# Seven half-size products in place of eight in a feed-forward up projection

## The chip, the cores and the metric

The kernel runs on one core of one Trainium2 chip. The metric is the device time of one launch in microseconds (us), the median of several runs. Lower is better.

## The reference, cut to what matters

The program is two transformer blocks on 512 tokens with 1024 features, in float32. The second block has two layers, and each layer ends with a feed-forward part:

```python
h = x + mixed @ w_out
f = jnp.square(jax.nn.relu(rmsnorm(h, norm2_g) @ w_up)) @ w_down
return h + f
```

`w_up` is 1024 by 4096 and `w_down` 4096 by 1024. The up projection thus has 32 output chunks of 128 features, each a contraction over eight chunks of 128, for 512 tokens.

## The kernel before, in words

Activations lie with features on partitions, so a tensor of 1024 features is eight tiles of 128 x 512. Each float32 operand is split into two float32r parts, H (a rounded copy, made by ScalarE, L140) and L (the rest, made by VectorE, L141). A product of two operands takes three matmuls: H by H, H by L, L by H (`mm3`, L162 to L164).

A weight chunk is loaded by one DMA of 512 KB from SyncE's queue (L150) into one of three `wr` buffers, split into one of two `w` buffers, and multiplied (`gemm`): eight contraction chunks, 24 matmuls of 512 columns. In the feed-forward part (`ffn`), the residual times the norm's gain is split once (`gain_split`, L229 and L230) into eight `x` buffer pairs. The norm's factor `rs` comes from `rstd_tile`: squares on ScalarE (L195), their sums on VectorE (L196), a few small matmuls, and twelve small VectorE operations (L123 to L134). Four groups follow. A group has eight up outputs and then eight down outputs, which take the group's eight up outputs as their contraction. An up output is read from PSUM by VectorE with max and times `rs` (L1910), squared by ScalarE (L1911) and split into a `y` buffer pair. A down output is added to the residual by VectorE (L1917).

Before the feed-forward part stands an output projection (L1895) whose eight results are added to `h` one by one (L1896). Its operand `mixed` lies in the same eight `x` buffer pairs, so these come free chunk by chunk while the last of its eight outputs is multiplied.

Buffers of a name (`w2` has eight, `wr` three, `w` two, `x` and `y` eight pairs, `wg` six) are handed out in program order. A planner (the Tile layer) then orders each engine's instructions: among those that are ready in its own model of time, the one that stands first in the program goes first. On the chip each engine runs its list in that order and waits on semaphores.

Of the kernel before, what the change touches and what calls it, by code (L numbers as in the profile page):

```python
# [49 lines left out]
class Builder:  # L50
    """Pools, constants and the operations that the stages share.

    Activations lie with features on partitions: a tensor of 1024 features is
    eight tiles of [128, 512 tokens]."""

    def __init__(self, tc, d, ctx):
# [3 lines left out]
        # whether the split of weights goes before all other work  # L60
# [31 lines left out]
    def psg(self):  # L92
        """In turn one of three banks; of two where attention takes the third."""
# [9 lines left out]
    def consts(self):  # L103
# [8 lines left out]
        # tri[s, l] = 1 where s <= l  # L112
# [6 lines left out]
    def rsqrt(self, out, x, scale, eps):  # L119
        """out = (scale * x + eps) ** -0.5 by Newton's steps, for small tiles."""  # L120
# [35 lines left out]
    def mm3(self, ps, wH, wL, xs, start=True, stop=True):  # L156
        """ps (+)= w.T @ x over the chunks, each operand in two parts."""
        nc = self.nc
        n = len(xs)
        for k, (xH, xL) in enumerate(xs):  # L160
            s, e = start and k == 0, stop and k == n - 1
            nc.tensor.matmul(ps, wH[:, k], xH, start=s, stop=False)  # L162
            nc.tensor.matmul(ps, wH[:, k], xL, start=False, stop=False)  # L163
            nc.tensor.matmul(ps, wL[:, k], xH, start=False, stop=e)  # L164
# [9 lines left out]
    def colsum(self, ps, acc, n=T):  # L174
        """ps[:, tb] = the sum over partitions of acc, tokens on partitions."""
# [4 lines left out]
    def rowbc(self, ps, col, n=T):  # L180
        """ps[p, t] = col[t % 128, t // 128] on every partition."""
# [17 lines left out]
    def rstd_rows(self, srcs, width, eps=EPS, n=T, w2=None, pss=None):  # L199
        """A PSUM tile with the tokens' reciprocal root mean squares on every partition."""  # L200
# [10 lines left out]
    def rstd_tile(self, srcs, width, eps=EPS, out=None):  # L211
        """The same on chip, until the next norm or in out."""
# [33 lines left out]
    def transpose4(self, ps, src, n=T):  # L246
        """ps[:, tb*128:...] = the transposes of src's blocks of 128 columns."""
# [5 lines left out]
    def causal_probs(self, score, mask, scale, pT):  # L253
        """The softmax of scale * (score + mask), keys on partitions: pT[k] holds for block k of
        keys the queries from that block on. score(ps, i) computes block i of queries against the
        keys up to it; mask[:, T - n:] is what is added to the last n keys up to a block's own."""
# [3 lines left out]
        def blocks(tile):  # L260
            # a block's columns in three tiles: the last, the first and third, the second
# [35 lines left out]
def fm(w):  # L297
    """[K, N] -> [N/128, 128, K/128, 128]: chunks of columns, contraction on partitions."""
# [8 lines left out]
def layout(x):  # L307
    """The program's arrays: the inputs, only laid out anew."""
# [12 lines left out]
    # S5: [(group parity, state), group pair, ...]  # L321
# [11 lines left out]
    # memory attention  # L333
# [3 lines left out]
    # PEER  # L337
# [4 lines left out]
    # second block  # L342
# [19 lines left out]
    # [layer, group of 8 chunks, out chunk, 128, 8, 128]  # L362
# [18 lines left out]
# columns of vec1  # L381
# [3 lines left out]
def exp_precise(B, out, x):  # L385
    """exp to float32's accuracy, for small tiles: 2**n times a polynomial."""
# [25 lines left out]
def pieces(x, bits, n):  # L412
    """x as a sum of float constants of few bits each, so that a product with a count is exact."""
# [13 lines left out]
def reduce_angle(B, x, tmp):  # L427
    """x - 2 pi round(x / 2 pi), within [-pi, pi]."""
# [31 lines left out]
def cmul(B, or_, oi, ar, ai, br, bi, t, neg_i=False):  # L460
    """(or_, oi) = (ar + i ai)(br + i bi); with neg_i the imaginary part is negated."""
# [14 lines left out]
class S5:  # L476
    """The state-space mixer: 8 steps of 64 chunks; (step, channel) on partitions for a
    group's input and output, (group parity, state) for the states. The groups go in
    quarters of 8, one tile of features each."""

    def __init__(self, B, pool):
# [15 lines left out]
        # powers 0..8  # L497
# [9 lines left out]
        # decay of eight steps; rotations of 8, 16, .. 256 steps  # L507
# [11 lines left out]
        # the factor of the input matrices, (A - 1) / lambda  # L519
# [14 lines left out]
    def matrices(self, q):  # L534
        """What a quarter's groups need of the parameters."""
# [25 lines left out]
        # output matrices C A^k, k = 0..8, the imaginary part negated  # L561
# [6 lines left out]
        # chunk inputs: A^(7-s) B, transposed to (step, channel) on partitions  # L568
# [13 lines left out]
        # kernels within a chunk: K_k[c', c] = Re(C A^k B), then laid out as a Toeplitz matrix  # L582
# [5 lines left out]
        # the two halves of the rows go to banks of their own  # L588
# [18 lines left out]
    def run(self, u, mats, outer):  # L607
        """u: a tile [(group, channel), (step, chunk)] -> gelu(y), laid out alike."""
# [17 lines left out]
        # rotate back, scan with real decays, rotate forth  # L626
# [35 lines left out]
def glu(B, yt, xs, vec):  # L662
    """Twice y * sigmoid(y @ w + b), in place."""
# [10 lines left out]
def glu_norm(B, yt, vec):  # L674
    """What glu gave, normalised; tokens back in their order; split."""
# [14 lines left out]
def attention_head(B, qT, kT, vt, h, out, pool):  # L690
    """A head of chunk-causal attention with a relative bias; out: the PSUM tile of its pair."""
# [3 lines left out]
    # the first chunk of a block doesn't see the second  # L695
# [13 lines left out]
def mixers(B, vec, memory, new_h):  # L709
    """The residual after the first block's mixers; memory() is a generator to run meanwhile."""  # L710
    nc, tc = B.nc, B.tc
    w = B.d["w_in"]
    with tc.tile_pool(name="mixers", bufs=1) as pool:
# [4 lines left out]
        # sel[k, n, p] = 1 where row k is the head of partition p in chunk n  # L718
# [12 lines left out]
        def ssm(p5):  # L731
# [42 lines left out]
        def pair(j):  # L774
            """The queries and keys of two heads, normalised."""
# [39 lines left out]
        def memories():  # L815
            # two steps a turn
# [22 lines left out]
        # the attention's part of the first products, meanwhile  # L839
# [22 lines left out]
def head_norms(B, raw, gains, per, width, n=T, w2=None, pss=None):  # L862
    """Scales each head's chunks (per of them) by its reciprocal root mean square and gains."""
# [17 lines left out]
def head_norm(B, raw, gains, width):  # L881
    """The same for one head; a generator."""
# [112 lines left out]
# products with experts' keys done while the gates are worked out  # L995
# [975 lines left out]
```

## Time and profile before

| what | value |
|---|---|
| median of 3 runs | 4764.99 us (4758.9 to 4768.86) |
| span of the profiled execution | 4766.1 us |
| TensorE busy | 4705.0 us (99%) |
| VectorE busy | 2838.4 us (60%) |
| ScalarE busy | 1907.6 us (40%) |

The span is what the chain of instructions takes in the one profiled execution; it lies 1.1 us above the median of the runs. [...]

### The profile page before, as it was taken

Reading aid. Unit: us, or ns where it says so; the run is one execution under the profiler, and the core shown is the slowest. Engines: PE = TensorE matmul, PEld = TensorE weight load, DVE = VectorE, ACT = ScalarE, POOL = GpSimd, SP = SyncE. Lnnn points to the kernel's source line nnn. Section 1 sums busy time; section 2 is a strip of 40 time slices with the busy share of each in tenths; the row PEclk is TensorE's granted clock in tenths of the full one; section 3 lists DMA queues with packets and bytes.
Section 4 is the critical chain, followed back from the end, with each engine's and each line's share of the span. In section 5 each row is a group of like instructions: output and inputs, shape, how many; then the busy total and the mean of one; then the engine's idle time right before and its main releaser. Section 6 shows DMA issues by size and latency. Waiting matters only on the chain.

```text
span 4766.1 us, 59356 instructions
## 1 busy us (share of the span) xinstructions
PE 4705.0 (99%) x22296; PEld 3754.0 (79%) x22296; DVE 2838.4 (60%) x5744; ACT 1907.6 (40%) x3653; POOL 29.1 (1%) x59
## 2 busy tenths in 40 slices
PE   8999999999999999999999999999999999999998
PEld 6777788888888888887787678888877876888887
DVE  8655799665545555557776545544477764555434
ACT  3343348863222222323553433333345534333322
POOL 0000000000000000000000000000000000000000
PEclk9789999999999999999999999999999999999999
DMA  4222235564434443442254145423323531554332
GB/s 131 66 84 83 80 118 186 190 210 150 138 119 139 143 129 126 145 138 74 85 178 137 45 154 175 146 93 96 104 81 127 174 103 52 176 167 133 93 95 82
DMA packets 306048, 589.28 MB, mean 124 GB/s; under 512 B 60192, under 2 KB 147552, under 8 KB 303584
## 3 DMA queue, kind: packets, MB, share of 16 engines
q1 hardware_dynamic: 304480, 582.88, 37.7%
q0 software_dynamic: 1280, 2.59, 0.3%
q8 instruction: 176, 2.88, 0.2%
q14 instruction: 112, 0.92, 0.1%
HBM read 480.29 MB, written 105.09 MB: 123 GB/s over the span
## 4 chain that ended last, share of the span: by engine, by line
PE 91%; DVE 6%; DMA 1%; issue 1%; ACT 0%; SPq 0%; DVEq 0%; ACTq 0%
PE g L162 14%; PE g L163 14%; PE g L164 14%; PE o L163 6%; PE o L164 6%; PE o L162 6%; PE s L1170 5%; PE s L1171 5%; PE s L1169 5%; PE s L1116 3%; PE s L249 1%; DVE wL L141 1%; PE s L1575 1%; PE s L1574 1%; PE s L183 1%
## 5 line engine op out<-in xcount | busy, mean ns | idle before, releaser
L140 ACT ACTIVATE wH<-wr 128x1024 fp32r<-128x1024 f32 (+2 forms) x599 | 603.3, 1007 | 1305.3 <-PE g L163 794.9
L141 DVE TENSOR_TENSOR wL<-wr,wH 128x1024 fp32r<-128x1024 f32 (+2 forms) x599 | 692.2, 1156 | 444.4 <-ACT wH L140 428.6
L162 PE MATMUL g<-xH,wH 128*128 128x512 f32 (+1 forms) x2328 | 923.4, 397 | 16.7 <-ACT wH L140 13.7
L164 PE MATMUL g<-xH,wL 128*128 128x512 f32 (+1 forms) x2328 | 919.9, 395 | 6.6 <-DVE wL L141 6.5
L163 PE MATMUL g<-xL,wH 128*128 128x512 f32 (+1 forms) x2328 | 922.2, 396 | 0.0
L162 PEld LDWEIGHTS g<-xH,wH 128*128 128x128 f32 x2328 | 444.7, 191 | 118.9 <-ACT wH L140 14.0
L164 PEld LDWEIGHTS g<-xH,wL 128*128 128x128 f32 x2328 | 444.4, 191 | 106.8 <-DVE wL L141 10.9
L163 PEld LDWEIGHTS g<-xL,wH 128*128 128x128 f32 x2328 | 444.7, 191 | 95.3 <-issue 3.7
L164 PE MATMUL o<-xH,wL 128*128 128x512 f32 x1032 | 411.2, 398 | 1.5 <-DVE wL L141 1.5
L163 PE MATMUL o<-xL,wH 128*128 128x512 f32 x1032 | 412.4, 400 | 0.0
L162 PE MATMUL o<-xH,wH 128*128 128x512 f32 x1032 | 411.2, 398 | 0.0
L1170 PE MATMUL s<-WL,VH 128*128 128x512 f32 x1024 | 399.7, 391 | 1.3 <-DVE WL L141 1.3
L1169 PE MATMUL s<-WH,VH 128*128 128x512 f32 x1024 | 398.2, 391 | 0.0
L1171 PE MATMUL s<-WH,VL 128*128 128x512 f32 x1024 | 397.7, 390 | 0.0
L140 ACT ACTIVATE VH<-vr 128x1024 fp32r<-128x1024 f32 x128 | 132.3, 1056 | 542.9 <-PE s L1170 391.4
L1172 DVE TENSOR_TENSOR h<-h,s 128x512 f32<-128x512 f32 x256 | 174.1, 685 | 271.6 <-PE s L1171 271.5
L164 PE MATMUL g<-yH,wL 128*128 128x512 f32 x632 | 251.0, 397 | 2.3 <-DVE wL L141 2.3
L163 PE MATMUL g<-yL,wH 128*128 128x512 f32 x632 | 251.1, 397 | 0.7 <-DVE yL L230 0.7
L162 PE MATMUL g<-yH,wH 128*128 128x512 f32 x632 | 250.5, 397 | 0.0
L141 DVE TENSOR_TENSOR VL<-vr,VH 128x1024 fp32r<-128x1024 f32 x128 | 154.1, 1224 | 141.4 <-ACT VH L140 141.3
L164 PEld LDWEIGHTS o<-xH,wL 128*128 128x128 f32 x1032 | 194.6, 189 | 45.2 <-DVE wL L141 2.4
L162 PEld LDWEIGHTS o<-xH,wH 128*128 128x128 f32 x1032 | 194.5, 188 | 44.5 <-issue 2.2
(629 smaller groups left out, 7243.3 us busy)
## 6 DMA issues: line engine op xcount, KB each, us to landing
wr<-in_w_in SPq DMA_DIRECT2D x166, 512.0 KB, 3.6
wr<-in_pu SPq DMA_DIRECT2D x128, 512.0 KB, 4.2
vr<-in_pv SPq DMA_DIRECT2D x128, 512.0 KB, 3.7
gd<-G SPq DMA_DIRECT2D x16, 2048.0 KB, 6.5
gt<-gd SPq DMA_DIRECT2D x64, 512.0 KB, 5.3
wr<-in_w_o SPq DMA_DIRECT2D x64, 512.0 KB, 3.6
wr<-in_w_up SPq DMA_DIRECT2D x64, 512.0 KB, 3.5
wr<-in_w_dn SPq DMA_DIRECT2D x64, 512.0 KB, 3.5
```

The source lines that it names most:

```text
L140: nc.scalar.activation(H, src, AF.Copy)
L141: nc.vector.tensor_tensor(L, src, f32(H), op=OP.subtract)
L162: nc.tensor.matmul(ps, wH[:, k], xH, start=s, stop=False)
L163: nc.tensor.matmul(ps, wH[:, k], xL, start=False, stop=False)
L164: nc.tensor.matmul(ps, wL[:, k], xH, start=False, stop=e)
L183: self.nc.tensor.matmul(ps[:, tb * P:(tb + 1) * P], col[:, tb:tb + 1].to_broadcast([P, P]), self.ident, start=True, stop=True)
L249: self.nc.tensor.transpose(ps[:, tb * P:(tb + 1) * P], src[:, tb * P:(tb + 1) * P], self.ident)
L1116: nc.tensor.matmul(ps[:, j * P:(j + 1) * P], o2[:, k], og[:, j], start=True, stop=True)
L1169: nc.tensor.matmul(ps, VH[:, n], WH, start=k == 0, stop=False)
L1170: nc.tensor.matmul(ps, VH[:, n], WL, start=False, stop=False)
L1171: nc.tensor.matmul(ps, VL[:, n], WH, start=False, stop=k == 3)
L1172: nc.vector.tensor_tensor(h[n], h[n], ps, op=OP.add)
```

## The change

The up projection goes two output chunks at a time (a pair). Seen as a 2 x 2 matrix of halves (outputs, contraction, tokens), a pair is eight products of half size. The change forms sums and differences of the quarters of the weights and of the operand and takes seven products (the Winograd form of Strassen's algorithm), whose sums give the four quarters of the result. `fast_moving` builds the operand's seven forms once for a layer. `fast_weights` builds the weights' four sums for each pair and splits seven half tiles. `fast_gemm` runs the seven products, each four contraction chunks of three matmuls of 256 columns: products 1, 3, 5 and 7 accumulate in PSUM bank x, 2 and 6 in bank y, 4 in bank z. Bank x is copied to SBUF by ScalarE after products 1, 3 and 5 (u0, u1, u2), and VectorE adds these copies to what lies in y and z. The down projection is as before. The rest of the textual change removes comments, so that line numbers shift.

```diff
+    def fast_moving(self, raws, main, extra):
...
+        for k in range(4):
+            r1, r2 = next(raws), next(raws)
+            t = self.w2(), self.w2()
+            t1, t2, t3, t4 = t[0][:, :n], t[0][:, n:], t[1][:, :n], t[1][:, n:]
+            v.tensor_tensor(t1, r1[:, n:], r1[:, :n], op=OP.subtract)
+            v.tensor_tensor(t3, r2[:, n:], r1[:, n:], op=OP.subtract)
+            v.tensor_tensor(t2, r2[:, n:], t1, op=OP.subtract)
+            v.tensor_tensor(t4, r2[:, :n], t2, op=OP.subtract)
+            A, Bt, E = main(), main(), extra()
+            for src, (H, L) in ((r1[:, :n], [x[:, :n] for x in A]), (t1, [x[:, n:] for x in A]),
+                                (r2, Bt), (t2, [x[:, :n] for x in E]), (t[1], [x[:, n:] for x in E])):
+                self.split(src, H, L)
...
+    def fast_weights(self, ap1, ap2, pool):
...
+            r.append(self.t([P, 8, P], F32, "wr", 3))
+            nc.sync.dma_start(r[-1], ap)
+        a11, a12, a21, a22 = r[0][:, :4], r[0][:, 4:], r[1][:, :4], r[1][:, 4:]
+        s = [self.w2().rearrange("p (k m) -> p k m", k=4) for _ in range(4)]
...
+            tag, home = (("w", None), ("v", pool))[i % 2]
+            H, L = (self.t([P, 8, P], F32R, tag + k, 2, home) for k in "HL")
...
+        v.tensor_tensor(s1, a21, a22, op=OP.add)
+        yield parts(0, a11, s1)
+        v.tensor_tensor(s2, s1, a11, op=OP.subtract)
+        yield parts(1, s2, a12)
+        v.tensor_tensor(s3, a11, a21, op=OP.subtract)
+        v.tensor_tensor(s4, a12, s2, op=OP.subtract)
+        yield parts(2, s3, s4)
+        yield parts(3, a22)
+
+    def fast_gemm(self, ap1, ap2, forms, part, tile, pool):
...
+        x, y, z = self.pss()[:, :n], self.pss()[:, :n], self.psg()[:, :n]
...
+        product(x, a, forms[0], True)
+        nc.scalar.copy(u[0], x)
+        product(y, b, forms[4], True)
+        a, b = next(w)
+        product(x, a, forms[5], False)
+        nc.scalar.copy(u[1], x)
+        product(z, b, forms[1], True)
+        v.tensor_tensor(c1[:, :n], z, u[0], op=OP.add)
+        a, b = next(w)
+        product(x, a, forms[6], False)
+        nc.scalar.copy(u[2], x)
+        v.tensor_tensor(c2[:, n:], y, u[2], op=OP.add)
+        (c,) = next(w)
+        product(y, b, forms[2], False)
+        v.tensor_tensor(c1[:, n:], y, u[1], op=OP.add)
+        product(x, c, forms[3], False)
+        return c1, (x, c2)
...
     def ffn(self, h):
...
-        xs = B.gain_split(h, vcol(self.vec, N2, 8), lambda: B.hl("x"))
+        with B.tc.tile_pool(name=f"ffn{self.l}", bufs=1) as pool:
+            self.ffn_in(h, pool)
...
+        def raws():
+            for k in (0, 4, 1, 5, 2, 6, 3, 7):
+                r = B.w2()
+                nc.scalar.activation(r, h[k], AF.Copy, scale=g8[k])
+                yield r
+        forms = B.fast_moving(raws(), lambda: B.hl("x"),
+                              lambda: [B.t([P, 3 * half], F32R, "xt" + k, 4, pool) for k in "HL"])
         rs = B.rstd_tile(h, 1024)
         for g in range(4):
             fs = []
-            for c in range(8):
-                ps = B.gemm(B.d["w_up2"][self.l, 8 * g + c], xs)
-                r, f = B.wg(), B.wg()
-                nc.vector.scalar_tensor_tensor(r, ps, 0.0, rs, op0=OP.max, op1=OP.mult)
-                nc.scalar.activation(f, r, AF.Square)
-                H, L = B.hl("y")
-                B.split(f, H, L)
-                fs.append((H, L))
+            for c in range(0, 8, 2):
+                w = [B.d["w_up2"][self.l, 8 * g + c + i] for i in range(2)]
+                c1, (x, c2) = B.fast_gemm(*w, forms, lambda: B.t([P, half], F32, "fu", 3, pool),
+                                           B.wg, pool)
+                for out, ps, sl in ((c1, c1, slice(0, T)), (c2, x, slice(0, half)),
+                                    (c2, c2[:, half:], slice(half, T))):
+                    nc.vector.scalar_tensor_tensor(out[:, sl], ps, 0.0, rs[:, sl], op0=OP.max, op1=OP.mult)
+                for r in (c1, c2):
+                    f = B.wg()
+                    nc.scalar.activation(f, r, AF.Square)
+                    H, L = B.hl("y")
+                    B.split(f, H, L)
+                    fs.append((H, L))
```

## Rows read from the trace of the kernel before

**Rows 1.** The page, part 1 (busy time by engine) and part 4 (chain by engine).
```profile
PE 4705.0 (99%) x22296; PEld 3754.0 (79%) x22296; DVE 2838.4 (60%) x5744; ACT 1907.6 (40%) x3653; POOL 29.1 (1%) x59
...
PE 91%; DVE 6%; DMA 1%; issue 1%; ACT 0%; SPq 0%; DVEq 0%; ACTq 0%
```

**Rows 2.** Windows: length, busy time of the engines, granted clock, DMA share, GB/s.
```profile
315.00:319.00 4.00, 4.00 (x19) 3.92 (x19) 0.00 (x0) 0.38 (x1) 0.00 (x0) 0.50 0.31 45
595.00:640.00 45.00, 44.70 (x218) 36.14 (x217) 44.59 (x251) 14.24 (x20) 0.00 (x0) 1.00 0.27 82
3120.00:3164.50 44.50, 44.50 (x196) 36.03 (x195) 20.67 (x27) 17.65 (x25) 0.00 (x0) 1.00 0.31 96
3164.50:3209.00 44.50, 44.50 (x193) 36.06 (x193) 15.31 (x16) 8.37 (x9) 0.00 (x0) 1.00 0.31 95
```

**Rows 3.** Timeline of PE: two matmuls of 512 columns, 24 matmuls apart.
```profile
3164.32 0.40 PE L162 MATMUL g<-yH,wH 128*128 128x512 f32 x1
...
3169.91 0.39 PE L162 MATMUL g<-yH,wH 128*128 128x512 f32 x1
```

**Rows 4.** Timeline of PE: matmuls of 256 columns, 15 matmuls apart.
```profile
302.42 0.28 PE L163 MATMUL g<-xL,wH 128*128 128x256 f32 x1
...
304.20 0.28 PE L163 MATMUL g<-xL,wH 128*128 128x256 f32 x1
```

**Rows 5.** Timeline of the weight loads of those matmuls, 15 loads apart.
```profile
302.42 0.19 PEld L164 LDWEIGHTS g<-xH,wL 128*128 128x128 f32 x1
...
304.20 0.19 PEld L164 LDWEIGHTS g<-xH,wL 128*128 128x128 f32 x1
```

**Rows 6.** Timeline of PE at a lower granted clock: 15 matmuls apart.
```profile
315.46 0.41 PE L163 MATMUL g<-xL,wH 128*128 128x256 f32 x1
...
318.66 0.41 PE L163 MATMUL g<-xL,wH 128*128 128x256 f32 x1
```

**Rows 7.** Timeline of DVE: three instructions that wait for nothing, 512 and 1024 columns.
```profile
3125.37 0.69 DVE L141 TENSOR_TENSOR yL<-wg,yH 128x512 fp32r<-128x512 f32 x1 [1.36 <-ACT yH L140]
3125.98 0.68 DVE L1910 SCALAR_TENSOR_TENSOR wg<-g,acc 128x512 f32<-128x512 f32 x1
3126.58 1.21 DVE L141 TENSOR_TENSOR wL<-wr,wH 128x1024 fp32r<-128x1024 f32 x1
```

**Rows 8.** Timeline of DVE: 256 columns, the first two reading PSUM.
```profile
171.52 0.41 DVE L633 TENSOR_TENSOR s5t<-s,roti 128x256 f32<-128x256 f32 x1
171.85 0.41 DVE L632 TENSOR_TENSOR s5t<-s,rotr 128x256 f32<-128x256 f32 x1
172.19 0.41 DVE L634 TENSOR_TENSOR s5t<-s5t,s5t 128x256 f32<-128x256 f32 x1
```

**Rows 9.** Timeline of ACT: instructions that follow at once.
```profile
3124.71 0.63 ACT L140 ACTIVATE yH<-wg 128x512 fp32r<-128x512 f32 x1
3125.25 1.06 ACT L140 ACTIVATE wH<-wr 128x1024 fp32r<-128x1024 f32 x1
```

**Rows 10.** Groups by form: ScalarE copies of 256 columns out of PSUM.
```profile
L919 ACT COPY wm<-g 128x256 f32<-128x256 f32 x8 | 2.9, 357 | 4.8 <-PE g L164 4.8
```

**Rows 11.** Timeline of DVE where the feed-forward part begins.
```profile
3103.26 0.68 DVE L196 TENSOR_TENSOR acc<-acc,w 128x512 f32<-128x512 f32 x1
...
3108.84 4.06 DVE L230 SCALAR_TENSOR_TENSOR xL<-h,vec,xH 128x512 fp32r<-128x512 f32 x6
3112.82 0.68 DVE L1896 TENSOR_TENSOR h<-h,o 128x512 f32<-128x512 f32 x1
...
3117.34 0.16 DVE L123 TENSOR_SCALAR sm<-s 128x4 f32<-128x4 f32 x1 [0.18 <-PE s L177]
3117.53 0.17 DVE L125 TENSOR_SCALAR sm<-sm 128x4 int32<-128x4 int32 x1
```

**Rows 12.** Timeline of PE there: the first matmul of the first up output.
```profile
3112.16 0.40 PE L162 MATMUL g<-xH,wH 128*128 128x512 f32 x1
```

**Rows 13.** DMA issues: KB each, us from issue to landing.
```profile
wr<-in_w_up SPq DMA_DIRECT2D x64, 512.0 KB, 3.5
```

More of the change, by code (lines that the diff above doesn't have):

```diff
@@ L154, in weight, with mm3 @@
         return H, L
-    def mm3(self, ps, wH, wL, xs, start=True, stop=True):
+    def mm3(self, ps, wH, wL, xs, start=True, stop=True, **more):
         nc = self.nc
@@ L161, in mm3 @@
             s, e = start and k == 0, stop and k == n - 1
-            nc.tensor.matmul(ps, wH[:, k], xH, start=s, stop=False)
-            nc.tensor.matmul(ps, wH[:, k], xL, start=False, stop=False)
-            nc.tensor.matmul(ps, wL[:, k], xH, start=False, stop=e)
+            nc.tensor.matmul(ps, wH[:, k], xH, start=s, stop=False, **more)
+            nc.tensor.matmul(ps, wH[:, k], xL, start=False, stop=False, **more)
+            nc.tensor.matmul(ps, wL[:, k], xH, start=False, stop=e, **more)
     def gemm(self, ap, xs, n=T, ps=None):
@@ L171, in gemm @@
         return ps
+    def fast_moving(self, raws, main, extra):
+        v, n = self.nc.vector, T // 2
+        forms = [[] for _ in range(7)]
+        raws = iter(raws)
+        for k in range(4):
[10 more added lines that the diff above has]
+                self.split(src, H, L)
+            two = lambda p, o: tuple(x[:, o:o + n] for x in p)
+            for f, x in zip(forms, (two(A, 0), two(Bt, 0), two(Bt, n), two(E, 2 * n), two(A, n),
+                                    two(E, 0), two(E, n))):
+                f.append(x)
+        return forms
@@ new lines, in fast_weights, with parts @@
+    def fast_weights(self, ap1, ap2, pool):
+        nc, v = self.nc, self.nc.vector
+        r = []
+        for ap in (ap1, ap2):
+            r.append(self.t([P, 8, P], F32, "wr", 3))
+            nc.sync.dma_start(r[-1], ap)
+        a11, a12, a21, a22 = r[0][:, :4], r[0][:, 4:], r[1][:, :4], r[1][:, 4:]
+        s = [self.w2().rearrange("p (k m) -> p k m", k=4) for _ in range(4)]
+        s1, s2, s3, s4 = s
+        def parts(i, *srcs):
+            tag, home = (("w", None), ("v", pool))[i % 2]
+            H, L = (self.t([P, 8, P], F32R, tag + k, 2, home) for k in "HL")
+            out = []
+            for i, src in enumerate(srcs):
+                sl = slice(4 * i, 4 * i + 4)
+                self.split(src, H[:, sl], L[:, sl])
+                out.append((H[:, sl], L[:, sl]))
+            return out
+        v.tensor_tensor(s1, a21, a22, op=OP.add)
[6 more added lines that the diff above has]
+        yield parts(3, a22)
@@ new lines, in fast_gemm, with product @@
+    def fast_gemm(self, ap1, ap2, forms, part, tile, pool):
+        nc, v, n = self.nc, self.nc.vector, T // 2
+        w = self.fast_weights(ap1, ap2, pool)
+        x, y, z = self.pss()[:, :n], self.pss()[:, :n], self.psg()[:, :n]
+        c1, c2 = tile(), tile()
+        u = part(), part(), part()
+        def product(ps, wt, form, start):
+            self.mm3(ps, *wt, form, start=start, skip_group_check=True)
+        a, b = next(w)
[7 more added lines that the diff above has]
+        v.tensor_tensor(c1[:, :n], z, u[0], op=OP.add)
+        a, b = next(w)
+        product(x, a, forms[6], False)
[6 more added lines that the diff above has]
+        return c1, (x, c2)
@@ L1902, in ffn, with ffn_in @@
         B, nc = self.B, self.B.nc
-        xs = B.gain_split(h, vcol(self.vec, N2, 8), lambda: B.hl("x"))
+        with B.tc.tile_pool(name=f"ffn{self.l}", bufs=1) as pool:
+            self.ffn_in(h, pool)
+    def ffn_in(self, h, pool):
+        B, nc = self.B, self.B.nc
+        g8 = vcol(self.vec, N2, 8)
+        half = T // 2
+        def raws():
[5 more added lines that the diff above has]
+                              lambda: [B.t([P, 3 * half], F32R, "xt" + k, 4, pool) for k in "HL"])
         rs = B.rstd_tile(h, 1024)
```

## The prediction

> **What bounds the kernel now.** The page comes first: TensorE is busy 99% of the span and has 91% of the chain that ended last, VectorE is busy 60% and ScalarE 40% [rows 1]. That is an average, so the windows of the stage come next. In a group's up part, 44.5 us long, TensorE never rests at full granted clock, VectorE is busy 20.67 us and ScalarE 17.65 us; in the down part VectorE has 15.31 us [rows 2]. The stage is bound by the pace of matmuls, and the other engines have half of their time to spare. The reader should see that this spare time is what the change spends. The pace itself is read from starts in the timeline: 24 matmuls of 512 columns take 5.59 us, one output [rows 3].
>
> **What TensorE gains.** A pair of outputs now costs 2 x 5.59 = 11.18 us. Afterwards it is 7 products x 12 matmuls = 84 matmuls of 256 columns. Such matmuls, each with a weight load of its own, stand in an early stage: 15 of them take 1.78 us, 0.1187 us each at the full granted clock [rows 4]. So a product takes 1.42 us and a pair 9.97 us. That is 1.21 us less than now: not an eighth, since half a matmul costs 0.119 and not half of 0.233. A group of four pairs would go from 44.7 to 39.9 us (4.8 us), and the eight groups of the two layers would gain 38.7 us if nothing else bound them.
>
> **What the weight loads cost.** The loads of those 256-column matmuls last 0.19 us each, but 15 of them also start within 1.78 us [rows 5]: they run beside the matmuls and each other, so I cost the doubled number of loads at nothing. [...]
>
> **What VectorE gets.** Records of VectorE overlap: instructions of 512 columns that wait for nothing start 0.605 us apart, though each record lasts 0.69 [rows 7]; those of 256 columns, PSUM operands among them, start 0.335 us apart [rows 8]. A pair needs four weight sums and seven L parts, 11 x 0.605 = 6.66 us ("preparation"), and three additions of 256 columns, one max-times-rs of 512 and two of 256, and two L parts of the outputs, 3 x 0.605 + 5 x 0.335 = 3.49 us ("evacuation"). Together that is 10.15 us against TensorE's 9.97: the two engines now tie within an up part, where before VectorE needed 20.67 / 4 = 5.2 us a pair. ScalarE needs 11 x 0.54 [rows 9] and three PSUM copies of 0.357 [rows 10], 7.0 us a pair: not the bound. The DMAs move the same bytes; a load lands in 3.5 us [rows 13], and two of a pair's loads wait for buffers that come free about a pair earlier, so I cost them at nothing too.
>
> [...] The rows show the full 0.69 in each record, but also the next start inside it, so I take 10.15, and keep 11.7 as a rival.
>
> **The three later groups of a layer.** During the last down outputs VectorE is mostly free, and the buffers (two `v`, one `w`, eight `w2`) let the next pair be prepared but for its third part (1.21 us). From the start of the up part until product 5 of the fourth pair can start, VectorE then owes the last residual addition 0.6 + 1.21 + 3 x (3.49 + 6.66) less the last quarter's L, which only product 7 needs (0.6): 31.7 us. TensorE gets there at 3 x 9.97 + 4 x 1.42 = 35.6 us. The slack is 3.9 us, 11%. Elsewhere VectorE is busy 44.59 of 45 us while TensorE runs through [rows 2], so TensorE should set the pace here, with small losses. One lies inside each pair: product 6 writes bank y, which the addition for c2 reads, which waits for the copy u2 after product 5. The end of a matmul's record after the next start (0.28 - 0.12), the copy 0.357 and the addition 0.41 make about 1.0 us with the hand-offs. It is covered if product 7, which waits for the copy alone, or product 1 of the next pair is put in between, and the planner does so where their parts are ready. I put all losses at 2.0 us a group, half a microsecond a pair (bounds: nothing, and 5.3 if every gap stays open and VectorE's waits add to it). Gain: 4.8 - 2.0 = 2.8 us a group.
>
> **The first group of a layer.** Here the work has no cover. The eight operand tiles share the `x` buffers with the output projection before them, so nothing can be written into them until its last output: now, six of the eight gain splits stand in one block from 3108.84 [rows 11], and the first up product follows at 3112.16 without a gap [rows 12]. The forms cost 4 x (4 x 0.335 + 3 x 0.335 + 2 x 0.605) = 14.2 us of VectorE, where six of the eight gain splits now take 4.06. Their raw tiles take `w2` buffers, eight of them, enough for two of the four steps; so before the last output begins only the differences and extra parts of two steps (2 x 2.28 us) can be done. The squares' sums of `rstd_tile` come after the forms in the program and take `w2` too, so they move from the output projection, where they are hidden now [rows 11], behind the forms: 7 x 0.605. The four weight sums wait behind those in turn. From about 3107.5, VectorE thus owes: forms 9.7, the last residual addition 0.6, squares' sums 4.2, twelve small instructions at 0.2 (2.4) [rows 11], four preparations less the first and the last quarter (25.4), three evacuations (10.5), in all 52.8 us until product 5 of the fourth pair. Products 5 to 7 take 4.27 us more, so the group's up part ends at 3164.6 with perfect packing, against 3112.16 + 44.7 = 3156.9 before: 7.7 us later. At 95% packing it is 10.5 us; some down matmuls can fill gaps in the last pair. I take 9.5 us a layer (bounds 7 and 13).
>
> **The sum.** 2 x 9.5 - 6 x 2.8 = +2.2 us on the profiled execution's 4766.1 us: 4768.3. Its span lies 1.1 us above the median of the runs, so I predict 4767 us. The gain of TensorE is real, but VectorE's new work takes it back where a layer's feed-forward part begins. A measurement here tells 0.2%, 9.5 us, from no change.
>
> **Rivals.**
> Faster, hidden beginning (chance 0.22). If the forms and squares' sums find room earlier than I think, or down matmuls fill the first group's gaps, the first groups gain like the later ones less about 4 us each: 8 x 2.8 - 8 = 14 us, or 38.7 - 8 = 31 us if there are no losses at all: 4735 to 4752 us. For it speaks that the planner now hides every wait here; against it, that buffers are handed out in program order.
> Slower, VectorE without overlap (0.12). If instructions with these waits take their whole records, 14 x 0.69 + 5 x 0.41 = 11.7 us a pair, all VectorE sums grow by 15.5%. The first group owes 52.8 x 1.155 = 61.0 us, 8.2 us more, which on top of 7.7 is about +16 a layer; the later groups need 36.6 us plus some 4 us of waits against 35.6, lose 5 and gain nothing: +33, 4798 us. It decides from about 11.2 us a pair. [...]
> Slower, open gap after product 5 (0.18). 1.0 us in each pair plus a loss of 0.8 us a group leaves the later groups at 4.8 - 4.8 = 0: +19, 4783 us.
> Slower, lower clock (0.06). [...]
> Slower, weight loads in the open (0.02). Loads of 0.19 us before each matmul would make 0.31 us each and 26 us a pair: 32 x 14.8 = +475 us, 5240 us. [...]
> The forecast has 0.40.
>
> **How the numbers follow.** The forecast's own range takes 7 to 13 us a layer for the first groups and 4.3 to 1 us for each later one: 14 - 26 = -12 to 26 - 6 = +20, 4753 to 4785, mostly within 9.5 us of now. Faster has the first rival and a little of the forecast: 0.25. Same has most of the forecast and the near end of two rivals: 0.39. Slower has the rest: 0.36. The range that leaves out 2 in 10 cuts the far half of the first rival and the far cases above: 4744 to 4794.
>
> **What the profile after would show.** Right: up matmuls starting 0.119 us apart; VectorE near 100% busy with TensorE waiting for it in the first up part of each layer, which ends 8 to 13 us later than before; later up parts of 41 to 43 us; squares' sums (one line) after 3112 us. Wrong: waits of TensorE on VectorE in the later groups, up parts over 44.5 us there, a first group without waits, or a granted clock below 1 in the stage.

## The result and the profile after

The changed kernel took 4793.65 us in the median of four runs (4788.38 to 4796.33), the kernel before 4765.25: a ratio of 1.0055, 95% interval 1.0038 to 1.0071. Six more runs of it later gave 4784.53 beside 4766.31, a ratio of 1.0034 (1.0022 to 1.0046). It is slower, by a third to a half of a per cent. The forecast was "the same" (4767 us); the range of 4744 to 4794 held the time, just.

In the table, a "first group" is the stretch of a layer from the seventh addition of its output projection to its first down addition, a "later group" the stretch from a group's first down addition to that of the next, and the whole feed-forward part reaches from the former to the last down addition. All are read from the starts of the additions in the timeline of VectorE.

| us | before | after | forecast |
|---|---|---|---|
| first group, layer 0 / 1 | 57.74 / 57.72 | 73.88 / 73.47 (+16.1, +15.8) | +9.5 each |
| later groups, six of them | 89.23 to 89.24 | 85.79 to 86.08 (-3.2 to -3.4) | -2.8 each |
| feed-forward part, layer 0 / 1 | 364.93 / 364.47 | 371.17 / 370.05 | |
| both parts together | | +11.8 | +2.2 |

First the page of the changed kernel, busy times and chain (PE is TensorE, PEld its weight loads, DVE VectorE, ACT ScalarE); TensorE's share of the chain was 91% before and VectorE's 6% [rows 1]:

```profile
PE 4691.3 (98%) x23448; PEld 3790.6 (79%) x23448; DVE 3026.4 (63%) x6216; ACT 2008.1 (42%) x3949; POOL 28.9 (1%) x59
...
PE 87%; DVE 8%; DMA 3%; issue 1%; ACT 1%; SPq 0%; DVEq 0%; ACTq 0%
```

TensorE's busy time fell by only 14 us (its records overlap: in the lines of a later group below they last 0.28 us and start 0.12 us apart), and VectorE's and the DMAs' shares of the chain grew. Where, the windows show (length, busy time of PE, PEld, DVE, ACT and POOL, granted clock, DMA share, GB/s): the last output of the projection, the start of the first up part cut finely, and in the last row the up part of the second group:

```profile
3112.50:3119.00 6.50, 6.50 (x30) 5.22 (x29) 5.58 (x14) 5.13 (x12) 0.00 (x0) 1.00 0.11 45
3119.00:3125.00 6.00, 2.57 (x14) 1.92 (x12) 6.00 (x16) 5.71 (x13) 0.00 (x0) 0.85 0.00 0
3125.00:3131.00 6.00, 0.31 (x2) 0.02 (x1) 5.97 (x11) 3.72 (x7) 0.00 (x0) 0.50 0.00 1
3131.00:3143.00 12.00, 6.34 (x29) 6.26 (x30) 8.33 (x23) 1.85 (x3) 0.00 (x0) 0.50 0.28 87
3143.00:3155.00 12.00, 12.00 (x96) 11.63 (x96) 7.00 (x13) 6.68 (x14) 0.00 (x0) 0.97 0.15 46
...
3227.00:3268.30 41.30, 41.30 (x335) 40.06 (x334) 34.39 (x64) 24.50 (x49) 0.00 (x0) 1.00 0.31 90
```

The later up part is as forecast: TensorE never rests, at full granted clock, for 41.3 us in place of 44.5 [rows 2], and none of the six later groups has a wait of TensorE in this profile. The first one is not. TensorE is busy 0.31 of 6 us, then 6.34 of 12 at a granted clock of 0.50. And VectorE, full until 3131, is then busy only 8.33 and 7.00 of 12 us: in these 24 us it is not VectorE's sum of work that holds TensorE back. What TensorE waits for around the first up part (us in total, times, the longest):

```profile
PE s L272 <- DVE acc L291: 7.5, 1, 7.5
PE s L278 <- DVE sm L134: 3.9, 1, 3.9
PE g L163 <- DVE xL L141: 3.1, 2, 2.4
PE g L162 <- ACT xH L140: 0.3, 1, 0.3
PE s L162 <- ACT fu L260: 0.3, 1, 0.3
```

L272 and L278 are the column sums and the row broadcast of the norm: four tiny matmuls each in the program, eight records each in the trace. In TensorE's timeline they stand between the first products:

```profile
3119.20 0.28 PE L162 MATMUL g<-xH,vH 128*128 128x256 f32 x1
...
3124.51 0.58 PE L163 MATMUL g<-xL,vH 128*128 128x256 f32 x1 [2.35 <-DVE xL L141]
3124.89 0.42 PE L164 MATMUL g<-xH,vL 128*128 128x256 f32 x1
3132.80 1.86 PE L272 MATMUL s<-ones,acc 128*128 128x1 f32 x8 [7.49 <-DVE acc L291]
3138.52 2.07 PE L278 MATMUL s<-ident,sm 128*128 128x128 f32 x8 [3.86 <-DVE sm L134]
3140.24 0.56 PE L162 MATMUL s<-xH,wH 128*128 128x256 f32 x1
...
3143.59 0.32 PE L162 MATMUL s<-xH,wH 128*128 128x256 f32 x1
3143.75 0.28 PE L163 MATMUL s<-xL,wH 128*128 128x256 f32 x1
```

The reader should see three things. Product 4 (into bank z, here named g) starts without a gap at 3119.20 and then stops for operand parts. Product 1 starts only at 3140.24, right behind the two norm steps. And from 3140.24 to 3143.59 the first 15 matmuls (product 1's twelve and three of product 2) start some 0.21 us apart, the pace that goes with a granted clock of 0.50 [rows 2, 6]; only then does it fall to 0.12.

Were product 1's operands there earlier? VectorE's timeline answers. The L part of its weights (`wL` from the loaded `wr`) was written at 3114.41 and the last L parts of the operand's quarters at 3123.44, two in 1.02 us: all was there by 3124.5. But the sums of squares (L291), with the next weight sums between them, end at 3132.7, and the reciprocal root (L123 to L134) takes from 3134.70 to 3138.47:

```profile
3114.41 0.68 DVE L141 TENSOR_TENSOR wL<-wr,wH 128x512 fp32r<-128x512 f32 x1
...
3123.44 1.02 DVE L141 TENSOR_TENSOR xL<-w,xH 128x256 fp32r<-128x256 f32 x2
...
3125.32 1.41 DVE L291 TENSOR_TENSOR acc<-acc,w 128x512 f32<-128x512 f32 x2
...
3132.06 0.68 DVE L291 TENSOR_TENSOR acc<-acc,w 128x512 f32<-128x512 f32 x1
3132.66 0.68 DVE L233 TENSOR_TENSOR w<-wr,w 128x512 f32<-128x512 f32 x1
3134.70 0.16 DVE L123 TENSOR_SCALAR sm<-s 128x4 f32<-128x4 f32 x1 [1.35 <-PE s L272]
...
3138.30 0.17 DVE L134 SCALAR_TENSOR_TENSOR sm<-sm,sm 128x4 f32<-128x4 f32 x1
```

So product 1 stood for 15.7 us behind two norm steps that it doesn't need. Before, the last sums of squares ran during the output projection, at 3103 us, and the first small instructions of the root at 3117 while TensorE multiplied [rows 11, 12]. Whether the late norm alone is the loss, or VectorE's backlog behind it, this profile can't say: that is what the experiments are for.

### The profile page after: what moved, and what is told of

The parts are those of the page before. It is cut to its first block, busy times and chain, and to the rows that moved or that the text cites. A ratio compares the mean times of both kernels' runs of the same rounds, so it can differ in the third digit from the quotient of the medians.

```text
span 4786.7 us, 62435 instructions
## 1 busy us (share of the span) xinstructions
PE 4691.3 (98%) x23448; PEld 3790.6 (79%) x23448; DVE 3026.4 (63%) x6216; ACT 2008.1 (42%) x3949; POOL 28.9 (1%) x59
## 4 chain that ended last, share of the span: by engine, by line
PE 87%; DVE 8%; DMA 3%; issue 1%; ACT 1%; SPq 0%; DVEq 0%; ACTq 0%
PE g L163 12%; PE g L164 12%; PE g L162 12%; PE o L162 5%; PE o L163 5%; PE o L164 5%; PE s L1265 5%; PE s L1266 4%; PE s L1264 4%; PE s L1211 3%; PE s L162 2%; PE s L163 2%; PE s L164 2%; DVE wL L141 2%; PE s L344 1%
## 5 line engine op out<-in xcount | busy, mean ns | idle before, releaser
L162 PE MATMUL g<-xH,wH 128*128 128x512 f32 (+1 forms) x1992 | 790.7, 397 | 16.4 <-ACT wH L140 13.4
L164 PE MATMUL g<-xH,wL 128*128 128x512 f32 (+1 forms) x1992 | 787.5, 396 | 7.8 <-DVE wL L141 7.8
L163 PE MATMUL g<-xL,wH 128*128 128x512 f32 (+1 forms) x1992 | 790.3, 397 | 0.0
L162 PEld LDWEIGHTS g<-xH,wH 128*128 128x128 f32 x1992 | 381.5, 192 | 103.8 <-ACT wH L140 13.7
L164 PEld LDWEIGHTS g<-xH,wL 128*128 128x128 f32 x1992 | 381.3, 191 | 94.0 <-DVE wL L141 12.6
L163 PE MATMUL o<-xL,wH 128*128 128x512 f32 x856 | 342.7, 400 | 0.0
L164 PE MATMUL o<-xH,wL 128*128 128x512 f32 x856 | 341.9, 399 | 0.3 <-DVE wL L141 0.3
L162 PE MATMUL o<-xH,wH 128*128 128x512 f32 x856 | 341.5, 399 | 0.0
L1265 PEld LDWEIGHTS s<-WL,VH 128*128 128x128 f32 x1024 | 192.2, 188 | 49.8 <-DVE WL L141 10.3
L1264 PEld LDWEIGHTS s<-WH,VH 128*128 128x128 f32 x1024 | 191.9, 188 | 45.7 <-ACT WH L140 5.0
```

The source lines that it names most:

```text
L162: nc.tensor.matmul(ps, wH[:, k], xH, start=s, stop=False, **more)
L163: nc.tensor.matmul(ps, wH[:, k], xL, start=False, stop=False, **more)
L164: nc.tensor.matmul(ps, wL[:, k], xH, start=False, stop=e, **more)
L1264: nc.tensor.matmul(ps, VH[:, n], WH, start=k == 0, stop=False)
L1265: nc.tensor.matmul(ps, VH[:, n], WL, start=False, stop=False)
```

## The experiments

All times are in us. "First" is the first group of layer 0 / layer 1; ratios are to runs of the kernel before on the same chip, with their 95% intervals.

| run | first | later (mean) | both feed-forward parts, to before | median | ratio |
|---|---|---|---|---|---|
| before | 57.7 / 57.7 | 89.2 | | 4765 to 4769 | |
| changed kernel | 73.9 / 73.5 | 85.8 | +11.8 | 4793.65 | 1.0055 (1.0038 to 1.0071) |
| e1_norm_late | 71.5 / 71.8 | 85.8 | +7.5 | 4779.19 | 1.0024 (1.0014 to 1.0034) |
| e2_norm_first | 64.0 / 64.6 | 85.8 | -6.9 | 4762.20 | 0.9993 (0.9983 to 1.0003) |
| e3_room | 74.4 / 74.0 | 85.8 | +13.1 | 4787.35 | 1.0037 (1.0024 to 1.0049) |
| e4_room_norm_first | 63.6 / 63.2 | 85.8 | -8.8 | 4764.11 | 0.9998 (0.9988 to 1.0007) |
| e5_split_norm | 69.6 / 69.0 | 85.9 | +3.2 | 4773.62 | 1.0018 (1.0009 to 1.0027) |
| e6_split_norm_room | 65.7 / 65.7 | 85.8 | -4.3 | 4765.83 | 0.9996 (0.9985 to 1.0006) |
| e7_dve_plus4 | 79.4 / 78.8 | 90.5 | +50.3 | 4823.43 | 1.0109 (1.0093 to 1.0124) |
| e8_before_again | 57.8 / 57.9 | 89.2 / 89.6 | +1.4 | 4770.97 | 1.0004 (0.9995 to 1.0013) |
| e9_eight_first8 | 57.6 / 57.6 | 85.8 | -20.5 | 4749.42 | 0.9961 (0.9947 to 0.9975) |
| e10_eight_first4 | 56.3 / 56.3 | 85.8 | -23.2 | 4746.79 | 0.9955 (0.9940 to 0.9970) |
| e11_eight_first2 | 64.0 / 64.0 | 86.0 | -6.6 | 4766.14 | 0.9993 (0.9984 to 1.0002) |
| e12_after_again | 73.1 / 72.8 | 85.9 | +10.9 | 4784.53 | 1.0034 (1.0022 to 1.0046) |

**The place of the norm.** In e1 the norm is asked for after the first pair's products:

```diff
-        rs = B.rstd_tile(h, 1024)
+        rs = None
...
+                rs = B.rstd_tile(h, 1024) if rs is None else rs
```

> The changed kernel, with the norm's factor asked for after the first pair's products instead of before them: the same instructions, another place in the program. Theory 1 (the order on TensorE: product 1 stands behind the norm's column sums and row broadcast, whose input is late, and TensorE's clock falls meanwhile): product 1 starts some 10 us earlier in each layer, so about 20 us less than the changed kernel, near 4774 us. Theory 2 (the prediction's: VectorE's total work sets the first group's end, whatever the order): the work is the same, so within 4 us of the changed kernel, 4790 to 4797.

Measured: 2.4 and 1.7 us less in the first groups, no more. Two lines of TensorE in e1:

```profile
3118.43 0.29 PE L162 MATMUL s<-xH,wH 128*128 128x256 f32 x1
...
3145.55 2.07 PE L278 MATMUL s<-ident,sm 128*128 128x128 f32 x8 [2.51 <-DVE sm L134]
```

Product 1 did get past the norm: it starts at 3118.43, right behind the projection, 21 us earlier than in the changed kernel, counted from the seventh addition. But the time is lost behind it. TensorE waits at nine places, 9.9 us in all, the longest 2.5 us (still the row broadcast, now ahead of the next products), and is busy 20 of the 30 us from 3118 on, with the granted clock at 0.50 in the last six. The median is nearer to theory 1's, and its first step came true, but what it should bring, products that only had to be let past, was not borne out.

In e2 the norm is asked for before the forms, in buffers (`wg`) that the forms don't use:

```diff
+        cs, ps = B.pss(), B.pss()
+        acc = B.sumsq(h, w2=B.wg)
+        B.colsum(cs, acc)
+        r = B.small([P, T // P])
+        B.rsqrt(r, cs[:, :T // P], 1.0 / 1024, EPS)
+        B.rowbc(ps, r)
+        nc.scalar.copy(acc, ps)
+        rs = acc
         forms = B.fast_moving(raws(), lambda: B.hl("x"),
...
-        rs = B.rstd_tile(h, 1024)
```

> The changed kernel, with the norm's factor asked for before the operand's forms and its squares in the wg buffers, which are free there: the sums of squares are hidden in the output projection again. Theory 1 (order on TensorE): the norm's matmuls have their input some 8 us earlier, so product 1 starts that much earlier in each layer: 12 to 18 us less than the changed kernel, 4776 to 4782. Theory 2 (VectorE's total work): 4.2 us of VectorE less in each first group: 8 us less, about 4785.

Measured: 9.9 and 8.9 us less in the first groups, more than either theory gave. The waits and the timeline of TensorE in e2:

```profile
PE g L163 <- DVE xL L141: 5.2, 2, 3.7
PE s L278 <- DVE sm L134: 1.0, 1, 1.0
PE s L162 <- ACT fu L255: 0.3, 1, 0.3
```

```profile
3115.21 1.05 PE L272 MATMUL s<-ones,acc 128*128 128x1 f32 x8
3116.13 0.36 PE L162 MATMUL g<-xH,vH 128*128 128x256 f32 x1
3120.24 0.58 PE L163 MATMUL g<-xL,vH 128*128 128x256 f32 x1 [3.75 <-DVE xL L141]
3120.62 0.41 PE L164 MATMUL g<-xH,vL 128*128 128x256 f32 x1
3122.07 2.08 PE L278 MATMUL s<-ident,sm 128*128 128x128 f32 x8 [1.04 <-DVE sm L134]
```

The column sums no longer wait, and the row broadcast waits 1.0 us. What is left is a wait for the operand's own L parts, with VectorE full (6.00 of 6 us from 3118) and the granted clock at 0.50 there. The first group is still 6 to 7 us longer than before. This edit moves two things at once: the place of the norm's small matmuls, and the 4.2 us of squares' sums, which run during the output projection again.

**Room for the forms.** e3 puts the raw halves and the first pair's weight sums into free `y` buffers instead of `w2`; e4 does both this and the early norm:

```diff
-                r = B.w2()
+                r = B.t([P, T], F32, "yH", 8)
...
-        s = [self.w2().rearrange("p (k m) -> p k m", k=4) for _ in range(4)]
+        own = (lambda: self.t([P, T], F32, "yL", 8)) if first else self.w2
+        s = [own().rearrange("p (k m) -> p k m", k=4) for _ in range(4)]
```

> The changed kernel, with the raw tiles of the forms in the yH buffers and the first pair's weight sums in the yL buffers, both free there, so that the forms of three steps and the first weight sums need not wait for w2 buffers; the norm stays behind them. Theory 1 (order on TensorE): the norm's matmuls still stand first and get their input 3 to 5 us earlier: 6 to 10 us less than the changed kernel. Theory 2 (VectorE's total work): some 6 us of VectorE in each layer go before the last output projection: 10 to 13 us less, 4781 to 4784.

> The second and third edit together. Theory 1 and theory 2 both say the most here: product 1 starts within some 4 us of the output projection's end. Theory 1: 24 to 30 us less than the changed kernel (4764 to 4770). Theory 2: 18 to 22 us less (4772 to 4776). If the later groups' gain of 3.4 us each is real, a kernel without any loss in the first groups would be some 20 us faster than the kernel before.

Measured: e3 gains nothing (74.4 and 74.0), e4 hardly anything over e2 (0.4 and 1.4 us in the groups, nothing in the median). e4's median lies at the edge of theory 1's range, but by the early norm alone. Buffers of `w2` were not what the first group waited for in these two.

**The norm in two parts.** If the queue order is the whole loss, the sums of squares early and the two small steps late should free it:

```diff
+        acc = B.sumsq(h, w2=B.wg)
         forms = B.fast_moving(raws(), lambda: B.hl("x"),
...
-        rs = B.rstd_tile(h, 1024)
+        rs = None
+        def factor():      # column sums, root, row broadcast from acc
...
+                rs = factor() if rs is None else rs
```

> The seven products stay; the norm is split in two. The squares and their sums are asked for before the forms are built, and the column sums, the reciprocal root and the row broadcast only after the first pair's seven products, so that nothing that waits for the norm stands ahead of the first pair in TensorE's queue. Theory 1 (what was lost in the first group of a layer was lost to the norm's two small matmuls, which stood in TensorE's queue ahead of products that could have run, and to the lower clock after it): that group, 73.9 and 73.5 us with seven products and 57.7 before, comes to 57 to 62 us, both feed-forward parts together to 13 to 20 us less than before, and the time to 4746 to 4756 us. Theory 2 (VectorE's work in that group is too much wherever the norm is asked for, as the prediction's sum had it): TensorE waits for forms and weight sums instead, the group stays at 63 us or more as with the norm asked for first, and the time at 4762 us or more.

> The split norm, and besides the raw halves of tokens go to free tiles of the next activations and the first pair's weight sums to free tiles of the low parts, so that neither waits for a buffer that an earlier step still holds. Theory 1 (the queue order is all that was lost): the same time as with the split norm alone, within 2 us. A rival (room for the forms is the next thing that is late once the queue is free): 3 to 6 us less over the two layers than with the split norm alone, in the first group of each layer.

Measured: theory 1 fell. The first groups stay at 69 us (e5) and 65.7 (e6, with the room of e3). Room, which had given nothing in e3 and e4, gives 7.5 us over the two layers here, more than its rival's 3 to 6. No single wait is left in e5, but nine of 0.2 us or more, 7.5 us in all: for the root, for H and L parts of the weights, and for those of the operand.

```profile
PE s L278 <- DVE sm L134: 2.1, 1, 2.1
PE s L162 <- ACT wH L140: 1.4, 1, 1.4
PE s L163 <- DVE xL L141: 1.3, 1, 1.3
PE g L162 <- ACT vH L140: 1.0, 2, 0.6
PE g L163 <- DVE xL L141: 0.8, 2, 0.6
PE g L162 <- ACT xH L140: 0.7, 1, 0.7
PE s L162 <- ACT fu L251: 0.2, 1, 0.2
```

Beside these waits the granted clock is at 0.50 from 3117.2 to 3123.2 and at 0.69 in the 6 us after, and the twelve small instructions of the root stretch from 3126.28 to 3135.83, among VectorE's other work. So with seven products throughout, the first group stays some 5.5 us or more longer than before wherever the norm stands, and what TensorE waits for is then mostly the engines that prepare the operands. My picture after e2, a queue that only had to be put right, was too simple.

**Cover for the forms.** The next three kernels give the forms something to hide behind: the first 8, 4 or 2 outputs of each layer go back to eight products, and the forms are built behind these. The norm is then asked for where the kernel before has it, so cover and norm change together. The core of the edit, here for 4:

```diff
+        xs = B.gain_split(h, g8, lambda: B.hl("x"))
         rs = B.rstd_tile(h, 1024)
...
+            by8 = 4 if g == 0 else 0
+            for c in range(by8):
+                ps = B.gemm(B.d["w_up2"][self.l, 8 * g + c], xs)
...
+                for k in {0: (0,), 1: (1, 2), 2: (3,)}.get(c, ()):
+                    add_form(k)
+            for k in range(4 if g == 0 else 0):
+                B.split(late[:, k], *[x[:, half:] for x in xs[k]])
+            for c in range(by8, 8, 2):
```

> The first group of each layer goes back to eight products (eight outputs of 24 matmuls of 512 columns, with the operands split as before, and the norm asked for where it was before); the sums and forms for the seven products are built in between, behind its outputs, and the three later groups use them. Theory 1 (the first group lost because its forms and norm had nothing to hide behind, and the later groups gain whatever goes before): first group 57.7 to 59 us, later groups 85.8, 10 us less for each layer's feed-forward part than before, 4744 to 4750 us. Rival (the forms' work is paid wherever it is put, since VectorE is then late for the down projection or for the next group's weights): first group or second group longer by 4 us or more, 4755 us or more.

> Only the first four outputs of a layer's first group by eight products, its last two pairs by seven, with the forms built behind those four outputs. TensorE then has 2 x 1.21 = 2.4 us less in the first group than with eight outputs. By the prediction's way of counting VectorE (all that it owes against all that TensorE has until product 5 of the last pair), it owes about 10.5 (forms) + 10.4 (two pairs by eight) + 12.7 (two preparations) + 3.5 (an evacuation) + 2.4 (small ones), 39.5 us, by 38 us: nearly a tie, first group 56 to 58.5 us, 4741 to 4750 us in all. If only what stands ahead of the first product counts, 55.3 to 56 us for the group, 4739 to 4744 us.

> Only the first pair of a layer by eight products, the forms built behind it, the other three pairs by seven. TensorE has 3 x 1.21 = 3.6 us less than with eight outputs. By the prediction's way of counting, VectorE owes about 10.5 + 5.2 + 19.4 + 7 + 2.4 = 44.5 us by 11.2 + 2 x 9.97 + 5.7 = 36.8 us: the group ends some 4 to 5 us later than before, 61 to 63 us, 4750 to 4758 us in all. If only what stands ahead of the first product counts (the norm and its place in the queue), the first pair hides it, and the group takes 54.2 to 57 us, 4736 to 4745 us in all.

Measured: e9 came out as theory 1 said, 57.6 us for the first group and 85.8 for the later ones, 0.39% less than before. In e10 VectorE is full, yet TensorE waits nowhere; the first group takes 56.3 us, within the range of the count and 0.3 us above the other one's, so that this run hardly tells the two apart. Its windows, from the last projection output to the end of the up part:

```profile
3111.00:3122.00 11.00, 11.00 (x54) 9.07 (x53) 10.14 (x19) 9.65 (x17) 0.00 (x0) 1.00 0.17 48
3122.00:3133.00 11.00, 11.00 (x53) 8.91 (x52) 10.98 (x31) 9.93 (x18) 0.00 (x0) 1.00 0.44 125
3133.00:3140.50 7.50, 7.50 (x35) 6.13 (x34) 7.38 (x18) 5.33 (x12) 0.00 (x0) 1.00 0.08 30
3140.50:3162.00 21.50, 21.50 (x171) 20.57 (x170) 19.73 (x37) 13.02 (x25) 0.00 (x0) 1.00 0.35 114
```

With one pair less of cover, e11 breaks: 64.0 us, 1 us above the 61 to 63 of the count (and a median of 4766, 8 us above its range). The timeline of TensorE and the windows of the same stretch in e11:

```profile
3129.26 0.28 PE L163 MATMUL s<-xL,wH 128*128 128x256 f32 x1
3136.68 0.58 PE L164 MATMUL s<-xH,wL 128*128 128x256 f32 x1 [7.14 <-DVE wL L141]
3137.05 0.41 PE L162 MATMUL s<-xH,wH 128*128 128x256 f32 x1
```

```profile
3121.80:3127.80 6.00, 6.00 (x31) 4.99 (x30) 6.00 (x23) 5.46 (x12) 0.00 (x0) 1.00 0.32 87
3127.80:3133.80 6.00, 1.74 (x12) 1.36 (x10) 6.00 (x15) 5.90 (x12) 0.00 (x0) 1.00 0.00 1
3133.80:3139.80 6.00, 3.12 (x14) 3.12 (x15) 6.00 (x12) 2.36 (x6) 0.00 (x0) 0.56 0.01 3
3139.80:3145.80 6.00, 6.00 (x47) 6.00 (x46) 4.87 (x9) 3.35 (x7) 0.00 (x0) 0.87 0.52 176
```

The excess is one wait of 7.14 us in the first fast product, for the L part of its weights, with VectorE full throughout, and then a lower clock (0.56, then 0.87). Here the norm's row broadcast was done before (at 3127.32), so this is the backlog by itself.

**VectorE's slack in the later groups.** e7 does each of the four weight sums twice, nothing left out:

```diff
         v.tensor_tensor(s1, a21, a22, op=OP.add)
+        v.tensor_tensor(s1, a21, a22, op=OP.add)
...
+        v.tensor_tensor(s2, s1, a11, op=OP.subtract)
...
+        v.tensor_tensor(s3, a11, a21, op=OP.subtract)
+        v.tensor_tensor(s4, a12, s2, op=OP.subtract)
```

> The seven products with each of the four chained sums of the weights done twice over (nothing left out, the same values written twice): 4 x 0.605 = 2.42 us more of VectorE for each pair, 9.7 us for each group. Theory 1 (VectorE and TensorE are nearly tied in the later groups, as the prediction had it: 31.7 us owed by 35.6): a group then owes 41.4, so 5.8 us more for each of the six later groups, 85.8 to about 91.6 us, and the first groups longer too: 4828 to 4845 us. Theory 2 (VectorE has room in the part of the down projections that the sum did not count): a later group grows by less than 2 us, and the time is 4795 to 4812 us.

Measured: the six later groups take 89.7 to 91.0 us, 4.7 more in the mean, and the median of 4823 lies 5 us below theory 1's range. Of 9.7 us added, 5.0 do not show in the group. But not all of the 9.7 fell into the up part. The last of the first pair's eight sums stands ahead of the group's last residual addition:

```profile
3320.51 0.68 DVE L237 TENSOR_TENSOR w<-wr,w 128x512 f32<-128x512 f32 x1
...
3323.03 0.69 DVE L2036 TENSOR_TENSOR h<-h,o 128x512 f32<-128x512 f32 x1 [1.23 <-PE o L164]
```

So the sums of three pairs, 7.3 us, were added there. By the prediction's own count, which leaves the first pair's third part for the up part, it would be 3 x 2.42 + 1.21 = 8.5 us, and 8.5 - 3.9 = 4.6: theory 1 holds, and the slack is not larger than the 3.9 us counted.

**The kernels again.** Both kernels unchanged, for a second profile:

> The kernel before once more, nothing changed, for a second profile of it: how much do stretches whose instruction order is the same differ between two profiled executions? If the 7 us by which the part ahead of the first feed-forward differed is chance, this profile differs from the first one there by several us too; if it belongs to the changed kernel, by less than 2 us. The feed-forward groups should repeat within 0.3 us (57.7 and 89.2).

> The changed kernel once more, nothing edited, for a second profile and more runs: of the 28 us between the first medians, the feed-forward parts hold 11.8 us. If the rest is chance of the executions, the ratio to the kernel before falls towards 1.0025 to 1.004 (4777 to 4784 us beside 4765) and the stretch ahead of the first feed-forward part, 3125.1 us in the first profile and 3114 to 3118 in two of the kernel before, moves by some us. If it belongs to the changed kernel, the ratio stays at 1.005 or more and the stretch at 3123 us or more. The feed-forward parts repeat within 1 us (371.2 and 370.1) in both cases.

Measured: the seventh addition of layer 0's output projection, which stands ahead of the change, started at 3106.8 and 3102.8 us of the span in the two profiles of the kernel before, and at 3113.8 and 3106.2 in those of the changed kernel (the texts above count from some 11 us earlier). The first groups of the changed kernel repeat within 0.8 us, with waits of 7.7 and 3.8 us at L272 and L278. So executions of one kernel differ there by 4 to 8 us, and the 7 us of the first pair of profiles can't be put down to the change. The feed-forward parts hold 11 to 12 us of the change; the ratios give 16 to 26. The rest lies outside these parts, and it may not be all chance: in the twelve profiles of kernels with some form of the change the addition starts at 3105.8 to 3115.7, 3110.8 in the mean, and for all twelve the difference of the medians to the kernel before is more than the feed-forward parts give, by 1 to 17 us. Why, the runs don't show.

## Why the prediction came out so

**Right: the pace and the weight loads.** The products' matmuls start 0.12 us apart, two loads and two matmuls of 256 columns in place of one each for 512. One product in a later group (the first lines of this product and of the next, 12 matmuls apart):

```profile
3250.21 0.28 PE L162 MATMUL s<-xtH,vH 128*128 128x256 f32 x1
...
3251.65 0.28 PE L162 MATMUL o<-xH,vH 128*128 128x256 f32 x1
```

That is 1.44 us, 1.42 forecast. The loads of this product last 0.19 us each and start 0.12 us apart as well (in the timeline of the loads, twelve from 3250.10 to the next product's first at 3251.53). The rival of loads in the open (5240 us) is out: a load and its matmul take 0.12 us together, as before [rows 4, 5].

**Right, a little low: the later groups.** -3.4 us against -2.8. Eight down outputs take 8 x 5.60 = 44.8 of the 85.8 us, so an up part costs 41.0, 1.1 us more than perfect packing where I had allowed 2.0. TensorE waits nowhere in these groups, so the gap after product 5 was covered and the rival of the open gap (4783) is out; e7 shows no more slack than the 3.9 us counted. The rival of VectorE without overlap (4798) came near the time, and near its +16 a layer in the first groups, but for the wrong reason: VectorE's 512-column instructions still start 0.60 us apart in the lines above (3132.06, 3132.66), and the later groups gained.

**Wrong: the first group, +9.5 forecast (bounds 7 and 13), +16.1 and +15.8 measured.** The step that failed is the one that added up what "VectorE owes" until product 5 of the fourth pair and let the group end when that is paid. It treated VectorE's work as if any of it could be done at any time before the end, with VectorE near 100% busy; from 3131 to 3155 it is busy 15.33 of 24 us. The account of layer 0 by the lines above: the waits of TensorE are 7.5 + 3.9 + 3.1 + 0.3 + 0.3 = 15.1 us. The lower clock adds 3.35 - 15 x 0.119 = 1.6 in the 15 matmuls from product 1 on, about 1.0 in the row broadcast (2.07 against 1.05 for the same instructions at full clock in e11) and 0.8 in the column sums (1.86 against 1.05 in e2): 3.4. The seven products give back 3.4. That makes 15.1 of 16.1; the last microsecond is not accounted for.

Two causes are in the 16, and the experiments part them in the main:

- The late norm, some 9 to 10 us a layer (e2 against the changed kernel). I had seen that the sums of squares move behind the forms, and priced them: 4.2 + 2.4 us of VectorE. What I did not ask is who stands behind their consumers. The column sums and the row broadcast were in TensorE's queue ahead of product 1, so a late norm stopped TensorE twice, and VectorE, busy 8.33 of the next 12 us, did not use that time for what it owed. The order in that queue is not the whole of it: letting product 1 past gave back 2 us (e1), the squares' sums early besides 4 (e5); only the whole norm early gave 9 to 10. How these divide between the queue, the 4.2 us of sums and the lower clock, the runs don't show.
- VectorE's backlog, some 5.5 to 7 us a layer, which stays with the norm early (e2, e4) and with a pair of cover (e11). This is what the forecast meant. Counted to the end it gave the right order of size (e11: 61 to 63 against 64.0; e10: 56 to 58.5 against 56.3), and with the norm early the median came out near my forecast, 4762 to 4764. That nearness is in part luck: the feed-forward parts of e2 and e4 are at -6.9 and -8.8 us where the forecast had +2.2. And in e2 and e11 the backlog is paid in the first fast product, not at the end: what decides there is the cover that TensorE has until then.

The lower clock, which I gave 0.06 as a rival of its own and named as a sign of being wrong, came about with these waits, at 3.4 us in layer 0. The hidden beginning did not come about by itself; e9 and e10 show what it would have been worth, 20 to 23 us.

The sum: +2.2 forecast, +11.8 in the profile. The first groups were 12.9 us dearer than forecast and the six later ones 3.6 us cheaper. So one term makes the change clearly slower. That the range held the time is luck rather than mechanism: its upper end came from rivals (4783, 4798) whose causes did not occur, and the forecast's own 4753 to 4785 misses the first median and holds the second (4784.5) just.

## What to carry to other kernels

Add up what an engine owes by when its first consumer needs it, not by the end of the stage, and for every step that becomes late look up what stands behind its consumer in the queue of that engine. Here TensorE stood 11.4 us at two tiny steps of a norm, and product 1, its operands there by 3124.5, started behind them at 3140.24; asking for the norm early gave back 9 to 10 us a layer, while only letting products past gave 2. A method with a costly preparation can be mixed with the plain one: the first four outputs of a layer by eight products and the rest by seven took 4746.8 us beside 4768.1 (0.9955, 0.9940 to 0.9970), faster than both kernels, where seven everywhere was slower or, with the norm early, the same (0.9993).

## What the runs showed of the hardware

In the stretch where TensorE was busy 0.31 of 6 us its granted clock was at 0.50; it stayed there while TensorE was busy 6.34 of the next 12 us, and was at 0.97 over the 12 us after that, with TensorE busy throughout. At 0.50 the 256-column matmuls start 0.21 us apart, at 1.00 0.12. In e11 the clock was still 1.00 in a window with TensorE busy 1.74 of 6 us, and 0.56 in the next: there the price of the wait came after it. The first group of the changed kernel paid 3.4 us for that beyond the waits themselves. And two profiled executions with the same instructions ahead of the feed-forward part reached it 4 us (kernel before) and 7.6 us (changed kernel) apart; the cause is open.
